# Ending and beginning the sub-layers of a two-layer decoder token tile by token tile

## The chip, the core and the metric

The kernel runs on one core of a Trainium2 chip. Its time is the device time in microseconds (us) of one execution. The core has a matrix engine (TensorE, PE in the profile; its weight loads are PEld), a vector engine (VectorE, DVE), a scalar engine (ScalarE, ACT), GpSimd (POOL) and SyncE (SP), which here starts the loads of the weights. The engines run side by side and wait for each other by semaphores. TensorE's results go to PSUM, which has eight banks here: three of them take transposes and small products, five take accumulators.

## The reference

Two layers on 256 tokens of width 2048, all in f32. Every sub-layer is wrapped in the same way, and that wrapping is what the change is about:

```
for i in range(DEPTH):
    h = rms_norm(x, g[0])
    mix = mlstm_mixer(h, ...) if i == 0 else gdn_mixer(h, ...)
    x = x + rms_norm(mix, g[1])
    h = rms_norm(x, g[2])
    x = x + rms_norm(mem_cross_attn(h, k_m, v_m, w_xq[i], w_xo[i]), g[3])
    h = rms_norm(x, g[4])
    x = x + rms_norm(sq_relu_mlp(h, w_up[i], w_down[i]), g[5])
```

`rms_norm(x, g)` is x * rsqrt(mean(x*x) + 1e-6) * g over the 2048 columns of a token. The mixer of layer 0 is an mLSTM, that of layer 1 a gated DeltaNet (gdn); each ends in a product with its output weights (m_out, g_out). The cross attention has four heads of 128 over 256 fixed memory tokens (products xq and xo), the MLP computes relu(h @ w_up)^2 @ w_down with 8192 inner columns (up and down).

## The kernel before

The 256 tokens are two tiles of 128 (t = 0 and 1). The residual stream x lies token-major in four chunks `xk` of 512 columns, each with both tiles. What goes into a product is feature-major: 16 tiles `h` of 128 features, each with 256 tokens twice, a high part and the rest (low part), since an f32 product is made of three products of rounded operands: high by high, high by low, low by high.

Weights come in units of 512 rows by 512 columns (four blocks of 128 rows), in the order of a plan. SP loads a unit in two halves (`raw`), ACT rounds each half into `hi` (L89) and VectorE makes the rest `lo` (L90). A product takes the units one after the other; `take` has the next ones started some units ahead, and the scheduler places these casts among the other work of ACT and VectorE, by program order, by a priority offset (`ws.first`) and by `behind(a, b)`, which keeps instruction a after b on their engine. After that order is set, each engine runs its instructions strictly in it.

There are two kinds of products. `prod_tok` (L384 to L386) keeps tokens on the output partitions and 512 columns free: three matmuls of 512 columns for each block of 128 rows and token tile. `prod_feat` (L318, L319, or L322 to L324 in the narrow form) keeps features on the partitions and tokens free; `prod_tall` (L337 to L339) is the same with one column of 128 features at a time. xq, up, and gdn's gq and gk are feature-major, xo, down, m_out, g_out and gdn's gz are token-major. The narrow form of three matmuls of 256 columns is used for xq, gq and the first four blocks of up (`fresh`), since it needs the high part of h first; the wide form is one matmul of 512 columns and one of 256.

A sub-layer ends in `Post`. `take` receives each accumulator of the last product as it is ready: ACT squares it (L232, the sum goes to `ss`), VectorE multiplies by the gain g into `y` (L472, L479); with down and g_out an earlier part of the sum is added first (L455). After the last chunk of a token tile `rstd` makes 1/rms: a reduction, a root on ACT and a reciprocal (L485 to L491). Then `advance` begins the next sub-layer. For each of the four chunks `residual` (L496) adds y * r to xk for both tiles, `feed` transposes the chunk's eight 128 by 128 blocks into two PSUM banks (L214) and splits them into h, ACT the high part (L249, 256 columns: both tiles), VectorE the low part (L250), in the two banks in turn; then ACT squares xk for the next norm (L232, junk<-xk), and two weight units are cast in between. The scale 1/rms of the next norm isn't applied to h: it is applied to the results later.

`extra_unit` puts the second of the next product's first two units into tiles that are free at the time (`xw` in the profile). In gdn the products gq, gk and gz alternate for four groups of heads; gz's results for the later heads go through memory (z_d). In the last sub-layer the output is written from xk.

## Time and profile before

| what | before |
|---|---|
| median of 3 runs | 2910.2 us (2903.45 to 2910.87) |
| profiled execution, its time | 2910.01 us |
| span of the profiled execution | 2908.3 us |
| granted TensorE clock, mean | 0.994 |
| busy: PE / DVE / ACT / POOL | 2867.1 / 1758.4 / 1425.2 / 158.4 us |

The page gives busy times, the chain of work that ended last, and the costliest groups of instructions. A row of a group is line, engine, operation, output<-inputs, shape and count, then busy time and mean duration (ns) of one, then the engine's idle time before them and what ended it. A row of a timeline is start, duration, engine, line, operation, tiles, shape, count, and in brackets the idle time before it with its releaser. A row of the waits is who waited for whom, the sum in us, the times and the longest. A row of a table of stretches is the stretch, its length, the busy time (and count) of PE, PEld, DVE, ACT and POOL, the granted clock, and the DMA share and rate. A matmul's duration overlaps that of its neighbours, so its pace is read from starts.

### The profile page before, as it was taken

The page shows a single profiled execution, that of the slowest core. Times are in us where ns is not written, and L with a number is a line of the kernel's source. Part 1 is how long each engine was busy: PE and PEld are TensorE (multiplying, and loading weights), DVE is VectorE, ACT ScalarE, POOL GpSimd, SP SyncE. Part 2 cuts the span into 40 slices and gives each one's busy share as a digit, 9 for nine tenths or more (in the row PEclk, how much of TensorE's full clock was granted, in tenths as well). Part 3 has the DMA queues.
Part 4 walks back from the last instruction along what each step waited for, and adds up shares of the span by engine and source line. Part 5 has one row for each costly group of instructions (what it writes and reads, how often), then busy time and mean ns, then how long its engine had stood idle before and what let it go on. Part 6 is the DMA issues. An engine that isn't in the chain of part 4 may idle for free.

```text
span 2908.3 us, 42466 instructions
## 1 busy us (share of the span) xinstructions
PE 2867.1 (99%) x16683; PEld 2478.4 (85%) x16683; DVE 1758.4 (60%) x2603; ACT 1425.2 (49%) x2125; POOL 158.4 (5%) x341
## 2 busy tenths in 40 slices
PE   8999999999999999999999999999999999999998
PEld 7888888888888888798998998888888888888887
DVE  5555656654645555577776895555576545455565
ACT  6444546544434444466664554544465444344443
POOL 0000000000000000002211114230000000000000
PEclk9999999999999999999999999999999999999999
DMA  7645564555555565658778777664545555655554
GB/s 239 193 145 174 189 201 144 191 188 189 188 191 188 192 194 184 214 154 238 228 214 242 207 221 238 206 207 163 200 158 168 188 191 187 197 186 194 190 188 167
DMA packets 379515, 562.40 MB, mean 193 GB/s; under 512 B 24593, under 2 KB 158994, under 8 KB 376882
## 3 DMA queue, kind: packets, MB, share of 16 engines
q1 hardware_dynamic: 363456, 507.12, 55.6%
q0 software_dynamic: 14288, 51.23, 5.2%
q8 instruction: 131, 2.15, 0.3%
q10 hardware_dynamic: 1570, 1.33, 0.1%
q14 instruction: 70, 0.57, 0.1%
HBM read 534.37 MB, written 25.23 MB: 192 GB/s over the span
## 4 chain that ended last, share of the span: by engine, by line
PE 91%; DVE 4%; DMA 2%; ACT 2%; issue 1%; DVEq 0%; SPq 0%; ACTq 0%
PE up L318 15%; PE up L319 8%; PE down L385 8%; PE down L384 8%; PE down L386 8%; PE g_out L386 2%; PE g_out L384 2%; PE g_out L385 2%; PE o L318 2%; PE gz L384 2%; PE gz L386 2%; PE gz L385 2%; DMA raw<-in_gdn_w_in 1%; DVE lo L90 1%; PE o L319 1%; PE v L386 1%
## 5 line engine op out<-in xcount | busy, mean ns | idle before, releaser
L90 DVE TENSOR_TENSOR lo<-raw,hi 128x1024 fp32r<-128x1024 f32 x938 | 1110.3, 1218 | 890.3 <-ACT hi L89 888.8
L89 ACT CAST hi<-raw 128x1024 fp32r<-128x1024 f32 x938 | 943.3, 1046 | 953.5 <-PE down L386 310.8
L318 PE MATMUL up<-h,hi 128*128 128x512 f32 x1920 | 678.7, 399 | 0.0
L319 PE MATMUL up<-h,lo 128*128 128x256 f32 x1920 | 539.2, 281 | 0.0
L318 PEld LDWEIGHTS up<-h,hi 128*128 128x128 f32 x1920 | 360.8, 188 | 89.9
L385 PE MATMUL down<-lo,u 128*128 128x512 f32 x1024 | 398.4, 389 | 0.0
L384 PE MATMUL down<-hi,u 128*128 128x512 f32 x1024 | 398.4, 389 | 0.0
L386 PE MATMUL down<-hi,u 128*128 128x512 f32 x1024 | 398.3, 389 | 0.0
L319 PEld LDWEIGHTS up<-h,lo 128*128 128x128 f32 x1920 | 362.7, 189 | 0.2
L384 PEld LDWEIGHTS down<-hi,u 128*128 128x128 f32 x1024 | 192.2, 188 | 40.1
L386 PEld LDWEIGHTS down<-hi,u 128*128 128x128 f32 x1024 | 192.2, 188 | 40.0
L385 PEld LDWEIGHTS down<-lo,u 128*128 128x128 f32 x1024 | 192.2, 188 | 39.6
L337 PE MATMUL gv<-h,hi 128*128 128x256 f32 x512 | 146.4, 286 | 2.5 <-ACT hi L89 2.5
L339 PE MATMUL gv<-h,lo 128*128 128x256 f32 x512 | 145.9, 285 | 0.9 <-DVE lo L90 0.9
L338 PE MATMUL gv<-h,hi 128*128 128x256 f32 x512 | 145.4, 284 | 0.0
L384 PE MATMUL gz<-hi,h 128*128 128x512 f32 x256 | 104.6, 409 | 0.0
L385 PE MATMUL gz<-lo,h 128*128 128x512 f32 x256 | 102.8, 402 | 0.0
L386 PE MATMUL gz<-hi,h 128*128 128x512 f32 x256 | 102.7, 401 | 0.0
L337 PEld LDWEIGHTS gv<-h,hi 128*128 128x128 f32 x512 | 98.7, 193 | 3.0 <-ACT hi L89 2.7
L339 PEld LDWEIGHTS gv<-h,lo 128*128 128x128 f32 x512 | 98.7, 193 | 1.2 <-DVE lo L90 1.1
L338 PEld LDWEIGHTS gv<-h,hi 128*128 128x128 f32 x512 | 98.6, 193 | 0.2 <-issue 0.2
L889 DVE SCALAR_TENSOR_TENSOR cv<-pad,cols,cv 128x256 f32<-128x256 f32 x192 | 90.8, 481 | 6.9 <-ACT cv L887 4.2
(435 smaller groups left out, 4701.5 us busy)
## 6 DMA issues: line engine op xcount, KB each, us to landing
raw<-in_w_up SPq DMA_DIRECT2D x256, 512.0 KB, 4.0
raw<-in_w_down SPq DMA_DIRECT2D x256, 512.0 KB, 4.1
raw<-in_gdn_w_in SPq DMA_DIRECT2D x192, 512.0 KB, 4.9
raw<-in_mlstm_w_in SPq DMA_DIRECT2D x96, 512.0 KB, 4.0
raw<-in_gdn_w_out SPq DMA_DIRECT2D x64, 512.0 KB, 4.4
raw<-in_mlstm_w_out SPq DMA_DIRECT2D x32, 512.0 KB, 4.5
at_d<-at POOLq DMA_DIRECT2D x8, 1536.0 KB, 7.9
ab<-at_d POOLq DMA_DIRECT2D x8, 1536.0 KB, 8.4
```

Of the source, the lines that this page charges most:

```text
L89: a = nc.scalar.copy(h_, raw[:, :, :n])
L90: return a, nc.vector.tensor_tensor(l_, raw[:, :, :n], h_, ALU.subtract)
L318: PE.matmul(a[:fw], wh, srcs[kk][:, :], start=(kk == 0), stop=False, skip_group_check=True)
L319: PE.matmul(a[:fw, T:], wl, srcs[kk][:, 0:T], start=False, stop=(kk == nk - 1), skip_group_check=True)
L337: PE.matmul(a[:, 0:T], hi[k], srcs[k][:, 0:T], start=(k == 0), stop=False)
L338: PE.matmul(a[:, 0:T], hi[k], srcs[k][:, T:], start=False, stop=False)
L339: m = PE.matmul(a[:, 0:T], lo[k], srcs[k][:, 0:T], start=False, stop=(k == nk - 1))
L384: PE.matmul(accs[t], sh, hi[j], start=(kk == 0), stop=False)
L385: PE.matmul(accs[t], sh, lo[j], start=False, stop=False)
L386: PE.matmul(accs[t], sl, hi[j], start=False, stop=(kk == nk - 1))
L889: V.scalar_tensor_tensor(c, pad[:, j : j + T], w[j], c, ALU.mult, ALU.add)
```

## The change

`advance` is gone; its work is spread over the end of one product and the beginning of the next. The last two weight units of the ending product are run as a pair: token tile 0 through both, then tile 1 through both. When tile 0 is done, its 1/rms is made (one sum of the first three chunks is taken earlier, and the root reads the last square's sum with that as its bias), and two residuals follow. `ahead` puts the transposes and splits of chunk 0, tile 0 into the middle of the last unit of tile 1; then come the remaining weight cast and chunk 1, tile 0. The first product of the next sub-layer is token-major now (xq with 384 columns, up with its first 512 columns, gz in gdn, moved ahead of gq), and its first two units are a pair again; after each of its four parts `between` places more: chunk 0 of tile 1, chunk 1 of tile 1, chunk 2 of both, chunk 3 of both. The results of xq and of the first up columns are transposed afterwards (xqt, and `feed` of utok). `half` transposes the four blocks of a chunk and one tile into one bank and splits them in 128 columns each. `follow` fixes the order on ACT and VectorE around it. The eight squares of xk stand after the last split. Besides, weight casts get a priority offset of 60 around xo, the load of the root's table is asked for earlier, and the exponential of gdn's a_log stands behind the lead.

```diff
+        steps = [(c, k) for c in range(n_ch) for k in range(0, nk, UK)]
+        accs, units = {}, {}
+        def fetch(i):
+            c, k = steps[i]
+            if k == 0:
+                if start:
+                    start(c)
                 for t in range(2):
+                    accs[c, t] = acc(f"{key}{c}_{t}")
+            units[i] = ws.take(key, 1 if post and i == len(steps) - 1 or lead and i < 2 else None)
+        def run(i, t, j0=0, j1=UK):
+            c, k = steps[i]
+            hi, lo, kb, n = units[i]
+            a = accs[c, t][:, :n]
+            for j in range(j0, j1):
+                kk = k + j
+                sh, sl = srcs[kk][:, t * P : (t + 1) * P], srcs[kk][:, T + t * P : T + (t + 1) * P]
+                PE.matmul(a, sh, hi[j][:, :n], start=(kk == 0), stop=False)
+                PE.matmul(a, sh, lo[j][:, :n], start=False, stop=False)
+                PE.matmul(a, sl, hi[j][:, :n], start=False, stop=(kk == nk - 1))
+        def done(i, t):
+            c, k = steps[i]
+            if k + UK == nk:
+                evac(c, t, accs[c, t][:, : units[i][3]])
+        pairs, i = [], 0
+        while i < len(steps):
+            two = i == 0 and lead or i == len(steps) - 2 and (post or split)
+            pairs.append((i, i + 1) if two else (i,))
+            i += len(pairs[-1])
+        for p_ in pairs:
+            last = p_[-1] == len(steps) - 1
+            if post and last:
+                extra_unit(4 if nk == UK else 0)
+            for i in p_:
+                fetch(i)
             for t in range(2):
+                for i in p_:
+                    if t and i == p_[-1] and last and post:
+                        post.halves = ws.begin()
+                        run(i, t, 0, UK // 2)
+                        post.ahead()
+                        run(i, t, UK // 2)
+                    else:
+                        run(i, t)
+                    if lead and p_[0] == 0:
+                        lead.between(t * 2 + i)
+                    done(i, t)
+            if after:
+                for i in p_:
+                    after(steps[i][1] // UK)
...
+            if ch == 2:
+                p_ = self.pre[t] = small.tile([P, 1], F32, tag=f"pre{t}", name="pre")
+                self.later(V.tensor_reduce(p_, self.rms.ss[:, t, 0:3], AX.X, ALU.add))
+                V.scalar_tensor_tensor(p_, p_, 1.0 / D, self.bias[:, t : t + 1] if self.bias is not None else eps_t,
+                                       ALU.mult, ALU.add)
             if ch == 3:
-                self.r.append(self.rstd(t))
-                late = lambda: V.tensor_tensor(d, a, self.g[ch], ALU.mult)
-                if t == 0 and not plus:
-                    late()
-                else:
-                    self.late.append(late)
-                self.added = v if plus else None
+                r = self.r[t] = small.tile([P, 1], F32, tag=f"rpost{t}", name="rpost")
+                S.activation(r, self.rms.ss[:, t, 3:4], AF.Sqrt, bias=self.pre[t], scale=1.0 / D)
+                self.invert = lambda: V.reciprocal(r, r)
+                if not self.nxt or t == 0:
+                    self.invert()
+                self.late = lambda: V.tensor_tensor(d, a, self.g[ch], ALU.mult)
+                if self.nxt and t == 0:
+                    self.residual(0, 0)
+                    self.first = self.residual(1, 0)
+                    self.late()
...
+        def half(self, ch, t):
+            p_ = psum(f"lth{ch}")
+            for i in range(4):
+                PE.transpose(p_[:, i * P : (i + 1) * P], xk[ch][:, t, i * P : (i + 1) * P], ident)
+            for i in range(4):
+                kb = ch * 4 + i
+                if t == 0:
+                    self.h[kb] = acts.tile([P, 2 * T], F32R, tag=f"h{kb}", name=f"h{kb}")
+                g_, d, s_ = gain(*self.nxt, kb), self.h[kb], p_[:, i * P : (i + 1) * P]
+                a = S.activation(d[:, t * P : (t + 1) * P], s_, AF.Copy, scale=g_)
+                v = V.scalar_tensor_tensor(d[:, T + t * P : T + (t + 1) * P], s_, g_, d[:, t * P : (t + 1) * P],
+                                           ALU.mult, ALU.subtract)
+                self.follow(a, v)
+        def follow(self, a, v):
+            if self.last:
+                behind(a, self.last[0])
+                behind(v, self.last[1])
+            self.last = a, v
+        def both(self, ch):
+            for t in range(2):
+                behind(self.residual(ch, t), self.halved)
+            self.h[ch * 4 : ch * 4 + 4] = [acts.tile([P, 2 * T], F32R, tag=f"h{kb}", name=f"h{kb}")
+                                           for kb in range(ch * 4, ch * 4 + 4)]
+            return feed(xk[ch], ch, self.h, lambda k: gain(*self.nxt, k))
+        def ahead(self):
+            self.follow(*self.halves.pop(0)())
+            self.half(0, 0)
+        def advance(self):
+            if self.added:
+                behind(self.added, self.last[1])
+                self.last = self.last[0], self.added
+            for half in self.halves:
+                self.follow(*half())
+            self.half(1, 0)
+            self.x_rms = Rms("x")
+            return self
+        def between(self, i):
+            if i < 2:
+                if i == 0:
+                    behind(self.invert(), self.last[1])
+                behind(self.residual(i, 1), self.last[1])
+                self.half(i, 1)
+                if i == 1:
+                    self.halved = self.last[1]
+                    behind(self.late(), self.halved)
+                    ws.prefetch(1, self.follow)
+            elif i == 2:
+                self.both(2)
             else:
...
-        return h, rms
+                a, _ = self.both(3)
+                for ch in range(4):
+                    for t in range(2):
+                        behind(self.x_rms.add(xk[ch][:, t, :], t, ch), a)
...
+        qtok = [sc.tile([P, 384], F32, tag=f"qtok{t}", bufs=1, name="qtok") for t in range(2)]
+        prod_tok("xq", h, 1, lambda c, t, a: (V.tensor_copy, S.copy)[t](qtok[t], a), after=scales, lead=lead)
+        for f in range(XA_H - 1):
+            p_ = psum("xqt")
+            for t in range(2):
+                PE.transpose(p_[:, t * P : (t + 1) * P], qtok[t][:, f * P : (f + 1) * P], ident)
+            ev_q(f, Bank(p_, False))
...
+        S.sqrt(warm, sums[-1][:, 0:1])
+        ws.first = 60
+        lead = out_proj("xo", o, l, 3, (l, 4), True)
+        ws.first = 0
+        return lead
...
+        def first(ch, t, a):
+            S.activation(d[:, t, :], a, AF.Relu)
+            V.scalar_tensor_tensor(d[:, t, :], a, 0.0, d[:, t, :], ALU.max, ALU.mult)
         for c in range(NQ):
+            if c == 0:
+                prod_tok("up", h, 1, first, lead=lead)
             u = new_u()
-            prod_feat("up", h, KB, relu2(u), fresh=c == 0)
+            if c == 0:
+                feed(d, 0, u, lambda k: None)
+            prod_feat("up", h, KB, relu2(u), f0=0 if c else 4)
...
+            early_z(0, lead)
+            behind(S.activation(na, na, AF.Exp), lead.last[0])
...
-                early_z(c)
+                if c < 3:
+                    early_z(c + 1)
```

How it moves the instructions, first at the end of m_out in layer 0. On ACT before (junk<-m_out are the last squares of m_out's tiles 0 and 1, rpost the root, h the high parts from the banks ltp, junk<-xk the squares of x, hi74 and hi75 weight casts):

```order
L232 ACTIVATE junk_3851,sspost_3255<-m_out3_0_3697 128x512 [waits PE_49]
L487 ACTIVATE rpost_3855<-rpost_3855,eps_t_87 128x1 [waits DVE_49]
L232 ACTIVATE junk_3860,sspost_3255<-m_out3_1_3698 128x512 [waits PE_49]
L487 ACTIVATE rpost_3862<-rpost_3862,eps_t_87 128x1 [waits DVE_49]
L249 ACTIVATE h0_3868<-ltp0_3887,cols_98 128x256 [waits PE_49]
L249 ACTIVATE h2_3870<-ltp2_3888,cols_98 128x256 [waits PE_49]
L249 ACTIVATE h1_3869<-ltp0_3887,cols_98 128x256 [waits DVE_49]
L249 ACTIVATE h3_3871<-ltp2_3888,cols_98 128x256 [waits DVE_49]
L232 ACTIVATE junk_3906,ssx_3867<-xk0_108 128x512
L232 ACTIVATE junk_3908,ssx_3867<-xk0_108 128x512 [waits Activation_49]
L89 CAST hi74_3821<-raw74_2_3825 128x2x384 [waits DMAHW3_49]
L249 ACTIVATE h4_3872<-ltp4_3920,cols_98 128x256 [waits PE_49]
```

and now (lth is the bank of a half):

```order
L236 ACTIVATE junk_3827,sspost_3255<-m_out3_0_3703 128x512 [waits PE_49]
L503 ACTIVATE rpost_3829<-sspost_3255,pre_3681 128x1 [waits Activation_49]
L89 CAST hi74_3847<-raw74_0_3849 128x2x384 [waits DMAHW2_49,DVE_49,PE_49]
L536 ACTIVATE h0_3866<-lth0_3861,cols_98 128x128 [waits PE_49]
L536 ACTIVATE h1_3869<-lth0_3861,cols_98 128x128 [waits DVE_49]
L236 ACTIVATE junk_3884,sspost_3255<-m_out3_1_3704 128x512 [waits PE_49]
L536 ACTIVATE h2_3872<-lth0_3861,cols_98 128x128 [waits DVE_49]
L503 ACTIVATE rpost_3886<-sspost_3255,pre_3699 128x1 [waits Activation_49]
L536 ACTIVATE h3_3875<-lth0_3861,cols_98 128x128 [waits DVE_49]
L89 CAST hi74_3847<-raw74_2_3851 128x2x384 [waits DMAHW3_49]
L536 ACTIVATE h4_3895<-lth1_3890,cols_98 128x128 [waits PE_49]
L536 ACTIVATE h5_3898<-lth1_3890,cols_98 128x128 [waits DVE_49]
```

The splits are 128 columns wide and four to a bank, and each after the first of a bank waits for VectorE; the square and root of tile 1 stand among those of tile 0, and the squares of x are no longer between the chunks. On VectorE at the same place now (h are the low parts, xk the residuals):

```order
L507 TENSOR_TENSOR y3_3254<-m_out3_0_3703,g3_3551 128x512 [waits Activation_49]
L504 RECIPROCAL rpost_3829<-rpost_3829 128x1 [waits Activation_49]
L524 SCALAR_TENSOR_TENSOR xk0_108<-y0_3251,rpost_3829,xk0_108 128x512 [waits DVE_49]
L524 SCALAR_TENSOR_TENSOR xk1_109<-y1_3252,rpost_3829,xk1_109 128x512
L90 TENSOR_TENSOR lo74_3848<-raw74_0_3849,hi74_3847 128x2x384 [waits DMAHW2_49,Activation_49]
L537 SCALAR_TENSOR_TENSOR h0_3866<-lth0_3861,cols_98,h0_3866 128x128 [waits Activation_49]
L537 SCALAR_TENSOR_TENSOR h1_3869<-lth0_3861,cols_98,h1_3869 128x128 [waits Activation_49]
L537 SCALAR_TENSOR_TENSOR h2_3872<-lth0_3861,cols_98,h2_3872 128x128 [waits Activation_49]
L537 SCALAR_TENSOR_TENSOR h3_3875<-lth0_3861,cols_98,h3_3875 128x128 [waits Activation_49]
L90 TENSOR_TENSOR lo74_3848<-raw74_2_3851,hi74_3847 128x2x384 [waits DMAHW3_49,Activation_49]
L537 SCALAR_TENSOR_TENSOR h4_3895<-lth1_3890,cols_98,h4_3895 128x128 [waits Activation_49]
L537 SCALAR_TENSOR_TENSOR h5_3898<-lth1_3890,cols_98,h5_3898 128x128 [waits Activation_49]
```

Every low part waits for the high part of the same block on ACT; the two residuals of tile 0 come before the first of them.

The second place is the end of xo in layer 0, on ACT, where up's weight unit 86 is cast. Before (squares of the last chunks, the last splits h12 to h15, the casts of units 85 and 86):

```order
L232 ACTIVATE junk_4652,ssx_4553<-xk2_110 128x512 [waits Activation_49]
L232 ACTIVATE junk_4654,ssx_4553<-xk2_110 128x512 [waits Activation_49]
L89 CAST hi85_4804<-raw85_0_4806 128x1024 [waits DMAHW4_49,PE_49]
L249 ACTIVATE h12_4566<-ltp12_4657,cols_98 128x256 [waits PE_49]
L249 ACTIVATE h14_4568<-ltp14_4658,cols_98 128x256 [waits PE_49]
L89 CAST hi85_4804<-raw85_2_4808 128x1024 [waits DMAHW6_49]
L249 ACTIVATE h13_4567<-ltp12_4657,cols_98 128x256 [waits DVE_49]
L249 ACTIVATE h15_4569<-ltp14_4658,cols_98 128x256 [waits DVE_49]
L232 ACTIVATE junk_4675,ssx_4553<-xk3_111 128x512 [waits Activation_49]
L232 ACTIVATE junk_4677,ssx_4553<-xk3_111 128x512 [waits Activation_49]
L89 CAST hi86_4862<-raw86_0_4864 128x1024 [waits DMAHW7_49,PE_49]
L89 CAST hi86_4862<-raw86_2_4866 128x1024 [waits DMAHW0_49]
```

and now:

```order
L253 ACTIVATE h13_4709<-ltp12_4712,cols_98 128x256 [waits DVE_49]
L253 ACTIVATE h15_4711<-ltp14_4713,cols_98 128x256 [waits DVE_49]
L236 ACTIVATE junk_4730,ssx_4577<-xk0_108 128x512
L236 ACTIVATE junk_4732,ssx_4577<-xk0_108 128x512
L236 ACTIVATE junk_4734,ssx_4577<-xk1_109 128x512
L236 ACTIVATE junk_4736,ssx_4577<-xk1_109 128x512 [waits Activation_49]
L236 ACTIVATE junk_4738,ssx_4577<-xk2_110 128x512 [waits Activation_49]
L236 ACTIVATE junk_4740,ssx_4577<-xk2_110 128x512 [waits Activation_49]
L236 ACTIVATE junk_4742,ssx_4577<-xk3_111 128x512 [waits Activation_49]
L236 ACTIVATE junk_4744,ssx_4577<-xk3_111 128x512 [waits Activation_49]
L89 CAST hi86_4780<-raw86_0_4782 128x1024 [waits DMAHW7_49,PE_49]
L89 CAST hi86_4780<-raw86_2_4784 128x1024 [waits DMAHW0_49]
```

The eight squares now stand one after the other behind the last split, and the cast of unit 86 behind all of them; before, they stood two by two behind the splits of their own chunk, four of them ahead of the rows shown.

174 lines of the change are left out of this document (55 added, 119 removed).

## The prediction

> **What bounds the kernel now.** I read the page first, then the waits, then the stretches around the places where one sub-layer hands over to the next. The busy times by engine and the chain that ended last:
>
> ```profile
> PE 2867.1 (99%) x16683; PEld 2478.4 (85%) x16683; DVE 1758.4 (60%) x2603; ACT 1425.2 (49%) x2125; POOL 158.4 (5%) x341
> ...
> PE 91%; DVE 4%; DMA 2%; ACT 2%; issue 1%; DVEq 0%; SPq 0%; ACTq 0%
> ```
>
> TensorE sets the time. The change touches its work little, so what counts is where TensorE stands still: 9% of the chain, and mostly at the hand-overs. Let T be the time since the moment at which 24 matmuls (5.44 us) of the ending product are left. The five inner hand-overs, each from T = 0 to the first matmul of what follows unchanged (A: m_out to xo, B: xo to the second block of up, C: down to gk, D: g_out to xo, E: as B in layer 1), by stretches:
>
> ```profile
> 447.63:489.99 42.36, 40.51 (x282) 37.93 (x281) 31.54 (x66) 27.88 (x66) 0.00 (x0) 0.96 0.50 152
> 510.94:546.16 35.22, 32.80 (x250) 30.91 (x248) 28.57 (x52) 24.84 (x56) 0.00 (x0) 1.00 0.58 183
> 1228.15:1264.54 36.39, 33.18 (x253) 31.29 (x252) 25.77 (x46) 21.56 (x48) 0.00 (x0) 1.00 0.53 158
> 2111.09:2154.34 43.25, 40.23 (x282) 37.40 (x281) 32.89 (x68) 27.89 (x65) 0.00 (x0) 0.96 0.49 151
> 2175.43:2211.62 36.19, 34.25 (x250) 32.35 (x249) 28.71 (x52) 24.98 (x57) 0.00 (x0) 0.95 0.56 179
> ```
>
> The first number is the length, then PE, PEld, DVE, ACT; the one before the last two is the granted clock. DVE and ACT are busy for 59 to 81% of these 35 to 43 us: they have no great reserve there. Now A on TensorE (start, length, idle before and its releaser):
>
> ```profile
> 449.67 0.39 PE L384 MATMUL m_out<-hi,u 128*128 128x512 f32 x1
> ...
> 453.07 0.60 PE L214 MATMUL ltp<-ident,xk 128*128 128x128 f32 x4
> 455.52 1.10 PE L214 MATMUL ltp<-ident,xk 128*128 128x128 f32 x6 [1.85 <-DVE xk L496]
> ...
> 457.75 0.41 PE L323 MATMUL xq<-h,xw 128*128 128x256 f32 x1
> 457.97 0.41 PE L324 MATMUL xq<-h,xw 128*128 128x256 f32 x1
> ...
> 461.03 0.28 PE L322 MATMUL xq<-h,xw 128*128 128x256 f32 x1
> 461.15 0.28 PE L323 MATMUL xq<-h,xw 128*128 128x256 f32 x1
> ...
> 479.74 0.47 PE L337 MATMUL xq<-h,hi 128*128 128x256 f32 x1
> ```
>
> From 449.67 to 453.07 stand 15 matmuls of 512 columns, 0.2267 us each. TensorE then waits 1.85 us for the residual xk. What it runs next starts every 0.22 us, and every 0.12 us from 461.03 on: half clock for four microseconds after the gap. A, D and E have this (0.96, 0.96, 0.95), B and C don't (1.00). ACT and VectorE in the same place:
>
> ```profile
> 453.27 0.60 ACT L232 ACTIVATE junk<-m_out 128x512 f32<-128x512 f32 x1 [1.52 <-PE m_out L386]
> 454.18 0.29 ACT L487 ACTIVATE rpost<-rpost,eps_t 128x1 f32<-128x1 f32 x1 [0.22 <-DVE rpost L485]
> 455.99 0.84 ACT L249 ACTIVATE h<-ltp,cols 128x256 fp32r<-128x256 f32 x2 [1.51 <-PE ltp L214]
> 457.02 0.87 ACT L249 ACTIVATE h<-ltp,cols 128x256 fp32r<-128x256 f32 x2 [0.19 <-DVE h L250]
> 457.78 0.62 ACT L232 ACTIVATE junk<-xk 128x512 f32<-128x512 f32 x1
> ```
>
> ```profile
> 456.50 0.87 DVE L250 SCALAR_TENSOR_TENSOR h<-ltp,cols,h 128x256 fp32r<-128x256 f32 x2 [0.38 <-ACT h L249]
> 457.52 0.88 DVE L250 SCALAR_TENSOR_TENSOR h<-ltp,cols,h 128x256 fp32r<-128x256 f32 x2 [0.15 <-ACT h L249]
> 458.32 0.68 DVE L472 TENSOR_TENSOR y<-m_out,g 128x512 f32<-128x512 f32 x1
> 458.92 1.40 DVE L496 SCALAR_TENSOR_TENSOR xk<-y,rpost,xk 128x512 f32<-128x512 f32 x2
> ```
>
> Splitting one 512-column chunk of both token tiles takes from 455.99 to 458.40, 2.4 us, because two PSUM banks go to and fro: while ACT reads one, VectorE reads the other. That the two wait for each other in one bank, both ways, is in the waits, with the gap of TensorE below them:
>
> ```profile
> ACT h L249 <- DVE h L250: 10.8, 18, 1.1
> DVE h L250 <- ACT h L249: 8.4, 25, 1.2
> PE ltp L214 <- DVE xk L496: 11.8, 9, 2.2
> ```
>
> **The change, part by part.** *The narrow splits.* For chunks 0 and 1 each token tile now has a half of its own: four transposes into one bank, and from it four times an ACT row and a VectorE row of 128 columns. Each next ACT row waits for the VectorE row before it, as the order shows. The profile of before has no such row of h, so I take other rows of that size from PSUM, beside the weight casts that stand in the same queues:
>
> ```profile
> L668 ACT ACTIVATE dm<-ep,mg 128x128 f32<-128x128 f32 x12 | 3.5, 366 | 3.2 <-PE ep L665 3.1
> L1226 DVE SCALAR_TENSOR_TENSOR zs<-op,ss,zs 128x128 f32<-128x128 f32 x64 | 17.7, 344 | 0.9
> L90 DVE TENSOR_TENSOR lo<-raw,hi 128x768 fp32r<-128x768 f32 x12 | 11.3, 956 | 5.4 <-ACT hi L89 5.1
> L90 DVE TENSOR_TENSOR lo<-raw,hi 128x1024 fp32r<-128x1024 f32 x938 | 1110.3, 1218 | 890.3 <-ACT hi L89 888.8
> L89 ACT CAST hi<-raw 128x1024 fp32r<-128x1024 f32 x938 | 943.3, 1046 | 953.5 <-PE down L386 310.8
> ```
>
> A step is 0.366 + 0.344 us and two hand-overs of about 0.035 (an ACT row of 0.47 from 455.99 ends at 456.46, VectorE starts at 456.50), 0.78 us. A half is four steps, 3.1 us; four halves 12.5 us, where two chunks took 4.8 in two banks. Bounds: 0.40 if the two overlapped, and 1.02 if a row of 128 cost as much as one of 256 (two L249/L250 rows of 0.47). I take 0.78, nearest in size; 16 steps in five hand-overs make 80 steps, so the ends are -30 and +19 us on the sum.
>
> *Hand-over A.* The early part gains: token tile 0 is normalised while TensorE still has tile 1 to do. The square (0.2 to 0.88 with its read-out), the root directly behind it (1.21), y3 (0.68), the reciprocal and the first residual (0.75) are through at T = 2.4, so the first transposes wait for nothing; they stand behind 18 matmuls, at 4.08. From there the halves set the pace: tile 0 of chunk 0, with the square and root of tile 1 in between on ACT, to 8.3; the rest of weight unit 74 and chunk 1 to 12.3; residual and chunk 0 of tile 1 to 16.9; residual and chunk 1 to 21.4. Then y3 0.68, two low parts of 0.95 that partly ran before, four residuals 2.7: 26.4. Chunks 2 and 3 as before, 5.8: 32.2. TensorE has 96 matmuls of 384 columns to lay under this (about 0.174 us each, midway between 0.12 and 0.2267: 16.7 us, 0.6 less than the 144 narrow ones of before) and waits at every half. Now comes what is late next: all eight squares of x stand on ACT behind the last split, 8 x 0.62 less a little overlap, 4.9 us, from about 31.6 to 36.5, and behind them the cast of weight unit 77 (1.0, to 37.5) and its low part on VectorE (1.2, to 38.8). The third xq product needs both. Before it began at 479.74, T = 32.1, so 6.7 us are lost, and six more transposes (0.11 each) add 0.7: **+7.4**. The same squares feed the scale of the softmax, so nothing behind can run past them.
>
> *B.* The same chain, with the wider up block (96 x 0.2267 = 21.8 us, 1.35 less than 192 x 0.12) beneath: last split at 35.3, TensorE through at 38.3, but the next block waits for unit 86, queued on ACT behind the squares (34.75 + 4.9 + 1.04 = 40.7; low part 41.97). TensorE goes on from about 41.5, with 8 more transposes (0.86) 42.3, against 35.2: **+7.1**. *E* likewise 42.3 against 36.2: **+6.1**. *D* as A with the additions of g_out's chunks, 50.0 against 43.25: **+6.8**. *C* begins with gz in place of gq, 1.4 us less work; the product ends at 39.8, then waits 1.1 for the reciprocal root behind two squares and a table load: 40.9 against 36.4 - 1.4 = 35.0, **+5.9**. Its store of z goes with it on POOL's queue (5% busy, nobody waits for it until the output gate). The exponential of a_log, put behind the lead, adds one table load on ACT after the splits; ACT's 49% hide it, at most 1.3 if not. In gdn the last head group loses gz as cover and has about 8 us of VectorE work under the v products: VectorE's 40% idle hides it; -2 to +2, I take 0.
>
> *Weights of xo.* The first two units are now cast earlier. What that can give is the stall in xo:
>
> ```profile
> 504.01 0.39 PE L386 MATMUL xo<-hi,u 128*128 128x512 f32 x1
> 504.54 0.73 PE L384 MATMUL xo<-hi,u 128*128 128x512 f32 x2
> 505.80 0.50 PE L385 MATMUL xo<-lo,u 128*128 128x512 f32 x1 [0.52 <-DVE lo L90]
> ```
>
> Three matmuls take from 504.01 to 505.80, 1.8 us where 0.7 is due, and the fourth is 0.11 longer than its neighbours' 0.39: -1.2, once in each layer, **-2.4**. *The output's tail* loses a reduction and a small product between the last square and the residuals (0.16 + 0.15 and two hand-overs of 0.1): **-0.5**.
>
> Sum: 7.4 + 7.1 + 5.9 + 6.8 + 6.1 - 2.4 - 0.5 = +30.4. Against the profiled execution's 2910.0 (the median of the runs is 2910.2) that is **2940 us**.
>
> **The clock.** I leave the half clock as it is in the rows: some 1.7 us in three of five hand-overs. The Trainium skill's "TensorE: Matmul & The Clock Gate", Part 1, says the clock halves after an idle window of about 3.4 us and needs as much activity to come back; in A 1.85 us of waiting, or 3.45 with the transposes on both sides, was followed by the slow rows, while B and C, with the same order of work, stayed at 1.00, so the rows agree on the length of the slow stretch and show no fixed trigger. By that rule a hand-over with matmuls in every window would never cool, and the sum would be 5 us lower.
>
> **Rivals.** *Overlap (no change).* If the 128-column rows overlap after all, each hand-over gets 6.2 us back: 2909. For it: only the order says that they don't. Against: the waits of 10.8 and 8.4 us in both directions.
>
> *The gaps decide (faster).* If the halves never hold TensorE and the squares aren't in the way, the 11.8 us of waiting for xk, 5 us of half clock and 2.9 us of xo and tail go, and 1 to 2 us of work: about 2888. It decides if a half takes under the 2.1 us of twelve 384-column matmuls that lie beside it. 3.1 speaks against it, and the reserve of ACT and VectorE too.
>
> *Only the feed.* If the casts of units 77 and 86 run before the squares, or the products hold enough other work, some 3.3 us of each hand-over drop out: 2940 - 17 = 2923. For it: TensorE has attention work in A and D. Against: on ACT the squares stand first.
>
> *A cold clock.* If waits at every half keep TensorE at half clock, the first products take 16.7 to 21.8 us more, less what they waited anyhow: A and D +5 over my sum, B, C and E +10, together 2980. For it: 0.22 us after a gap of 1.85. Against: C, 1.00 after its gaps.
>
> **How the numbers follow.** Forecast 0.59, only the feed 0.15, the gaps decide 0.12, overlap 0.08, cold clock 0.06. 0.3%, 8.7 us, is what can be told from no change here. Faster: 0.12. Same: overlap and a little of the feed's low side, 0.10. Slower: 0.78. The forecast's own range is 2926 to 2956. To leave out no more than 2 in 10 the low end goes to 2907, which takes in the feed and the overlap; the high end stays at 2957, short of the cold clock and about the dear step (2959).
>
> **What would show it.** Right: waits of the ACT h row on the VectorE h row in the new half, 2 us and more per half; ltp or lth transposes that no longer wait for xk; the third xq product and the second up block waiting for hi or lo behind eight squares in a row; stretches A to E some 6 to 7 us longer; no wait for lo in xo. Wrong: steps well under 0.78 us, TensorE busy through the halves, or a granted clock near 0.5 through the first product. It falls as a whole if the halves end before their matmuls need them.

## The result

The change made the kernel slower: 2942.0 us (median of 4 runs, 2939.7 to 2944.1) against 2908.1 us (4 runs, 2903.5 to 2910.9), a ratio of 1.0118 with a 95% interval of 1.0100 to 1.0135. The forecast was 2940, in a range of 2907 to 2957. The profiled execution of the changed kernel took 2942.3 us. Its page, busy times and chain of waits:

```profile
PE 2884.7 (98%) x16423; PEld 2465.4 (84%) x16423; DVE 1766.9 (60%) x2649; ACT 1437.6 (49%) x2163; POOL 158.4 (5%) x341
...
PE 88%; DVE 6%; ACT 3%; issue 1%; DMA 1%; DVEq 0%; ACTq 0%
```

TensorE's share of the chain fell from 91 to 88%, VectorE's and ACT's rose from 6 to 9% together: the time went into waits of TensorE for these two. To see where, both executions are cut at the same points: A from T = 0 at the end of m_out to T = 0 at the end of xo, D the same in layer 1; B from there to the first matmul of down, E the same in layer 1; C from T = 0 at the end of down to the second gq. Before, these stretches were 63.3, 103.1, 99.1, 64.3 and 104.0 us. The table of stretches after (stretch, length, busy PE, PEld, DVE, ACT, POOL, granted clock, DMA share, GB/s):

```profile
446.16:521.63 75.47, 67.45 (x331) 54.41 (x330) 48.27 (x94) 44.76 (x102) 0.20 (x4) 0.95 0.40 121
521.63:631.54 109.91, 104.23 (x542) 84.96 (x541) 69.55 (x117) 57.39 (x108) 0.00 (x0) 0.97 0.56 172
1245.69:1372.80 127.11, 119.93 (x710) 102.87 (x708) 81.21 (x153) 73.23 (x121) 7.46 (x18) 0.95 0.56 165
2127.13:2201.11 73.98, 65.51 (x331) 53.38 (x330) 49.42 (x96) 44.79 (x102) 0.00 (x0) 0.98 0.41 121
2201.11:2312.19 111.08, 105.40 (x543) 85.47 (x541) 69.98 (x117) 57.66 (x108) 0.00 (x0) 0.97 0.55 172
sum 497.55, PE 462.53 PEld 381.09 DVE 318.42 ACT 277.82 POOL 7.65; mean PE 92.51 PEld 76.22 DVE 63.68 ACT 55.56 POOL 1.53
```

and the sum of the same table before:

```profile
sum 433.82, PE 419.79 PEld 373.15 DVE 299.77 ACT 253.84 POOL 6.35; mean PE 83.96 PEld 74.63 DVE 59.95 ACT 50.77 POOL 1.27
```

After the change C holds one gz product more, which before came later: 96 matmuls at 0.2267 us, 21.8 us. Without it the five stretches take 475.8 us, 42 more than before: A +12.2, B +6.9, C +6.3, D +9.6, E +7.1. The rest of the kernel gave 10 us back: the middle of gdn, from the second gq on, about 7.7, the start of the kernel up to m_out's end 1.5 and the output's tail 0.5. The span grew by 32.2.

The halves, in hand-over A. Chunk 0 of token tile 1 on ACT, then what follows the last split (rows of ACT's timeline after):

```profile
459.95 0.37 ACT L536 ACTIVATE h<-lth,cols 128x128 fp32r<-128x128 f32 x1 [1.99 <-PE lth L530]
460.74 0.37 ACT L536 ACTIVATE h<-lth,cols 128x128 fp32r<-128x128 f32 x1 [0.42 <-DVE h L537]
...
478.80 0.62 ACT L236 ACTIVATE junk<-xk 128x512 f32<-128x512 f32 x1
...
483.09 0.61 ACT L236 ACTIVATE junk<-xk 128x512 f32<-128x512 f32 x1
...
483.70 1.03 ACT L89 CAST hi<-raw 128x1024 fp32r<-128x1024 f32 x1
...
485.77 0.47 ACT L848 COPY qtok<-xq 128x384 f32<-128x384 f32 x1
```

VectorE in the same half:

```profile
460.35 0.35 DVE L537 SCALAR_TENSOR_TENSOR h<-lth,cols,h 128x128 fp32r<-128x128 f32 x1 [1.15 <-ACT h L536]
461.14 0.35 DVE L537 SCALAR_TENSOR_TENSOR h<-lth,cols,h 128x128 fp32r<-128x128 f32 x1 [0.43 <-ACT h L536]
```

One row of 128 columns on ACT, one on VectorE, in turn: 0.79 us from one ACT row to the next, where 0.78 was forecast. Over the whole kernel, by groups and by waits:

```profile
L536 ACT ACTIVATE h<-lth,cols 128x128 fp32r<-128x128 f32 x80 | 29.4, 368 | 48.5 <-DVE h L537 26.4 <-PE lth L530 22.0
L537 DVE SCALAR_TENSOR_TENSOR h<-lth,cols,h 128x128 fp32r<-128x128 f32 x80 | 28.0, 350 | 38.9 <-ACT h L536 38.9
```

And TensorE at the end of the same hand-over (start, length, idle before and its releaser):

```profile
467.71 0.36 PE L386 MATMUL xq<-hi,h 128*128 128x384 f32 x1
470.63 1.95 PE L218 MATMUL ltp<-ident,xk 128*128 128x128 f32 x10 [2.55 <-DVE xk L524]
472.30 0.69 PE L384 MATMUL xq<-hi,h 128*128 128x384 f32 x1
...
484.78 0.39 PE L339 MATMUL xq<-h,hi 128*128 128x256 f32 x1 [1.47 <-ACT hi L89]
...
486.04 0.58 PE L341 MATMUL xq<-h,lo 128*128 128x256 f32 x1 [0.75 <-DVE lo L90]
...
488.13 0.41 PE L340 MATMUL xq<-h,hi 128*128 128x256 f32 x1
488.34 0.41 PE L341 MATMUL xq<-h,lo 128*128 128x256 f32 x1
...
489.18 1.02 PE L832 MATMUL xs<-kmT,xq 128*128 128x256 f32 x4
```

The reader sees three things here: a wait of 2.55 us for the residual of chunk 2; the forecast wait for weight unit 77 behind the eight squares (1.47 for hi, 0.75 for lo); and the first scores xs, which start at 489.18, that is T = 43.0, where before they started at T = 30.6 (478.20 in the trace of before). A wait of the first kind is TensorE's longest in each of the five hand-overs. Over the whole kernel:

```profile
PE ltp L218 <- DVE xk L524: 16.4, 6, 4.5
PE lth L530 <- DVE xk L524: 2.2, 7, 0.5
```

Before, TensorE waited 11.8 us for xk; now it waits 18.6, most of it ahead of chunk 2, 2.5 to 4.5 us in each hand-over.

### The profile page after: what moved, and what is told of

It is laid out like the page before. It is cut to its first block, busy times and chain, and to the rows that moved or that the text cites. A ratio compares the mean times of both kernels' runs of the same rounds, so it can differ in the third digit from the quotient of the medians.

```text
span 2940.5 us, 42023 instructions
## 1 busy us (share of the span) xinstructions
PE 2884.7 (98%) x16423; PEld 2465.4 (84%) x16423; DVE 1766.9 (60%) x2649; ACT 1437.6 (49%) x2163; POOL 158.4 (5%) x341
## 4 chain that ended last, share of the span: by engine, by line
PE 88%; DVE 6%; ACT 3%; issue 1%; DMA 1%; DVEq 0%; ACTq 0%
PE up L320 15%; PE down L386 8%; PE down L385 8%; PE down L384 8%; PE up L321 8%; PE g_out L386 2%; PE g_out L384 2%; DVE lo L90 2%; PE g_out L385 2%; PE o L320 2%; PE gz L384 2%; PE gz L386 2%; PE gz L385 2%; PE o L321 1%; PE v L386 1%
## 5 line engine op out<-in xcount | busy, mean ns | idle before, releaser
L386 PEld LDWEIGHTS down<-hi,u 128*128 128x128 f32 x1024 | 192.2, 188 | 39.9
L384 PE MATMUL gz<-hi,h 128*128 128x512 f32 x248 | 101.5, 409 | 0.5 <-ACT h L536 0.5
L386 PE MATMUL gz<-hi,h 128*128 128x512 f32 x248 | 99.4, 401 | 0.4 <-DVE h L537 0.4
```

The lines of the kernel that those rows point to most:

```text
L384: PE.matmul(a, sh, hi[j][:, :n], start=(kk == 0), stop=False)
L386: PE.matmul(a, sl, hi[j][:, :n], start=False, stop=(kk == nk - 1))
```

## The experiments

The kernel before ran beside each on the same chip: 2907.6 us (25 runs) with the first four, 2909.9 us (7 runs) with the last three. Stretches below are those of the table above, C without the additional gz product where there is one. Single executions of one kernel differ by up to 9 us on either side of the median, so stretches say where time lies, medians how much it is. The profiled execution of both edits was the fastest of its ten, 8.8 us under their median. The change itself was run only beside the kernel before at 2908.1 us; set against the kernel before that ran beside each, the gains of the last three over the change are some 2 us larger than the medians as they stand.

| us | A | B | C | D | E | sum | median |
|---|---|---|---|---|---|---|---|
| before | 63.3 | 103.1 | 99.1 | 64.3 | 104.0 | 433.8 | 2907.6, 2909.9 |
| the change | 75.5 | 109.9 | 105.3 | 74.0 | 111.1 | 475.8 | 2942.0 |
| two banks | 68.0 | 105.3 | 96.8 | 67.2 | 103.9 | 441.1 | 2906.5 |
| squares spread | 71.7 | 108.6 | 104.9 | 70.6 | 107.6 | 463.4 | 2928.8 |
| banks and squares | 63.8 | 103.5 | 94.2 | 64.0 | 103.6 | 429.1 | 2901.6 |
| xq copied by VectorE | 72.4 | 108.9 | 105.1 | 72.1 | 110.4 | 468.8 | 2932.6 |
| cast first | 72.9 | 109.0 | 105.7 | 72.8 | 110.1 | 470.5 | 2935.4 |
| all, early residuals | 61.8 | 102.2 | 96.3 | 64.0 | 100.9 | 425.2 | 2891.3 |

### A half in two banks

```diff
-            p_ = psum(f"lth{ch}")
-            for i in range(4):
-                PE.transpose(p_[:, i * P : (i + 1) * P], xk[ch][:, t, i * P : (i + 1) * P], ident)
+            p_ = [psum(f"lth{ch}{b}") for b in range(2)]
+            for i in (0, 2, 1, 3):
+                PE.transpose(p_[i % 2][:, i // 2 * P : (i // 2 + 1) * P], xk[ch][:, t, i * P : (i + 1) * P], ident)
...
-                g_, d, s_ = gain(*self.nxt, kb), self.h[kb], p_[:, i * P : (i + 1) * P]
+                g_, d, s_ = gain(*self.nxt, kb), self.h[kb], p_[i % 2][:, i // 2 * P : (i // 2 + 1) * P]
```

> The change as it is, but a half spreads its four blocks over two PSUM banks, so that ACT and VectorE can each read one. Theory (the to and fro in one bank is on the path): a half falls from 3.1 to 1.9 us (0.37 + 0.37 on ACT beside 0.35 on VectorE), four halves from 12.5 to 7.6; beside the first products' matmuls (2.1 us for twelve of 384 columns, 2.7 for twelve of 512) some 3.5 to 4.5 us of each of the five hand-overs come back: 2920 to 2925 us. Rival (only the squares and casts behind the feed hold TensorE): no more than 3 us in all, 2939 to 2942.

Measured: 2906.5 us (10 runs, 2902.7 to 2910.3), ratio to before 0.9995 (0.9985 to 1.0005). This one edit takes back 35 us, all that the change had lost, where 17 to 22 were expected. The five stretches still take 7 us more than before; what the change gained elsewhere, gdn's order above all, makes up for them. The same half on ACT:

```profile
459.18 0.62 ACT L536 ACTIVATE h<-lth,cols 128x128 fp32r<-128x128 f32 x2 [1.58 <-PE lth L530]
459.96 0.62 ACT L536 ACTIVATE h<-lth,cols 128x128 fp32r<-128x128 f32 x2 [0.16 <-DVE h L537]
```

and on VectorE:

```profile
459.58 0.61 DVE L537 SCALAR_TENSOR_TENSOR h<-lth,cols,h 128x128 fp32r<-128x128 f32 x2 [0.93 <-ACT h L536]
460.36 0.61 DVE L537 SCALAR_TENSOR_TENSOR h<-lth,cols,h 128x128 fp32r<-128x128 f32 x2 [0.18 <-ACT h L536]
```

Two rows in a row take 0.62 us, not two times 0.37, and the half lasts from 459.18 to 460.97, 1.8 us where it was 3.1 (459.95 to 463.06). Twenty halves make 26 us. The sum of the stretches fell by 34.7. Much of the remainder is likely the granted clock, which rose in all five stretches, from 0.95 to 0.97 in A and from 0.98 to 1.00 in D for two: 1 minus the clock, times the length, summed over the five, is 18 us after the change and 10 here, by which I estimate 8 us. No run separates it. The waits within the halves, who for whom, sum, times and longest:

```profile
DVE h L537 <- ACT h L536: 14.2, 30, 1.2
ACT h L536 <- DVE h L537: 5.5, 18, 1.0
```

Those of ACT for VectorE fell from 26.4 us, those the other way from 38.9. TensorE's wait for xk fell with them, from 16.4 and 2.2 us to

```profile
PE ltp L218 <- DVE xk L524: 9.3, 5, 2.0
```

The rival, that only what stands behind the feed counts, is out.

### The squares spread

```diff
...
+            self.square(0, 0)
+            self.square(1, 0)
...
+                if i == 0:
+                    self.square(0, 1)
...
+                    self.square(1, 1)
...
-                self.both(2)
+                a, _ = self.both(2)
+                for t in range(2):
+                    behind(self.x_rms.add(xk[2][:, t, :], t, 2), a)
...
-                for ch in range(4):
-                    for t in range(2):
-                        behind(self.x_rms.add(xk[ch][:, t, :], t, ch), a)
+                for t in range(2):
+                    behind(self.x_rms.add(xk[3][:, t, :], t, 3), a)
```

> The change as it is, but the squares of x stand where ACT waits: two behind the halves of token tile 0, one behind each half of tile 1, two behind the splits of chunk 2, and only the last two behind the last split. Theory (the casts of the next weight unit and the scale of the softmax wait behind eight squares): casts and scale come 3.7 us earlier in each of five hand-overs, 2924 to 2928 us. Rival (what follows would wait as long for something else): within 3 us of the change, 2939 to 2943.

Measured: 2928.8 us (4 runs, 2927.1 to 2931.2), ratio 1.0072 (1.0053 to 1.0092): 13 us under the change, just short of the 14 to 18 of the theory. The stretches fell by 12.4, A, D and E by 3.4 to 3.8, but B by 1.3 and C by 0.4. So the squares are on the path, and not evenly. In E the granted clock was 1.00 here and 0.97 in the change, 3% of 111 us, so most of E's 3.5 us may be the clock; B, the same place in the other layer, gained 1.3.

### Both edits

> Both edits together, two banks and spread squares. If the two waits stand one behind the other in the chain, their gains add: 2903 to 2911 us. If one hides the other, the better of the two alone, some 2920.

The two diffs together. Measured: 2901.6 us (10 runs, 2892.8 to 2905.1), ratio 0.9973 (0.9961 to 0.9985), 40 us under the change. The single edits gave 35 and 13, 48 together. By the medians the second edit is worth 4.9 us on top of the first, where it was worth 13 alone. The stretches fell by 34.7, 12.4 and 46.7, almost the sum, but this profiled execution was 8.8 us under the median of its runs, so its stretches look better than the kernel is. And that 2901.6 lies near the range for gains that add doesn't decide, for this range was made with 17 to 22 us for the first edit and not 35. So the second wait isn't wholly hidden by the first, as 2906.5 would have it, and it isn't wholly behind it either: some 8 us of it are gone once the halves are short. Why is open.

### Only gdn's gz products moved, on the kernel before

```diff
             for c in range(4):
                 ws.add("gq", g_in, 0, D, c * 512, 512, tall=c > 0)
+                if c == 0:
+                    ws.add("gz", g_in, 0, D, GDN_QKV + 2048, 512)
...
-                ws.add("gz", g_in, 0, D, GDN_QKV + 2048 + c * 512, 512)
+                if c < 3:
+                    ws.add("gz", g_in, 0, D, GDN_QKV + 2560 + c * 512, 512)
...
+                if c == 0:
+                    early_z(0)
                 prod_k(c)
...
-                early_z(c)
+                if c < 3:
+                    early_z(c + 1)
```

> The kernel before with one thing of the change: gdn's gz products move one place ahead (the first directly behind gq, so that none stands behind the fourth group's gk), all hand-overs as before. Theory from the two traces (the projections of gdn took 7.8 us less after the change because of this order): 2900 us, -8. Rival, the prediction's (VectorE's idle time hides the order either way): 2906 to 2910.

Measured: 2900.9 us (10 runs, 2896.8 to 2907.2), ratio 0.9979 (0.9967 to 0.9990): 6.8 us faster than before. This part of the change pays, and the prediction had it at nothing. The first lines of the edit move the loads of the weights with the products. Where the time went: all of gv (first row) and the fourth group's stretch (second row), before,

```profile
1564.60:1762.64 198.04, 193.29 (x1597) 192.38 (x1596) 163.11 (x262) 95.11 (x142) 22.85 (x60) 0.99 0.81 232
1488.47:1564.60 76.13, 76.13 (x529) 70.32 (x527) 54.89 (x86) 45.52 (x60) 12.91 (x30) 1.00 0.76 217
```

and in this kernel, the fourth group first:

```profile
1503.27:1552.42 49.15, 49.15 (x407) 48.62 (x405) 39.88 (x65) 33.33 (x45) 7.29 (x19) 1.00 0.85 233
1552.42:1750.10 197.68, 196.73 (x1624) 194.66 (x1622) 166.48 (x275) 97.04 (x145) 27.13 (x69) 1.00 0.79 232
```

The fourth group takes 76.1 - 21.8 - 49.2 = 5.2 us less, since work of its pairs now runs within gv (1624 against 1597 matmuls there), and gv is no longer for it: TensorE stood idle for 4.75 us in it before (198.04 - 193.29) and for 0.95 now. Near the end of gv before, the longest wait of ACT is 6.7 us for one transfer of gdn's weights; TensorE waited 2.5 us for hi and 0.9 for lo there, and its granted clock was 0.87 in the last 13 us. In this kernel the wait for hi is gone and the clock there was 1.00. Why that transfer ends better in the new order was not tried. The second group of heads also took 5.6 us less in this profiled execution (78.88 against 84.47, granted clock 1.00 against 0.96), but only 2.4 less in that of the change, so this part may be chance.

### xq copied out by VectorE alone

```diff
-        prod_tok("xq", h, 1, lambda c, t, a: (V.tensor_copy, S.copy)[t](qtok[t], a), after=scales, lead=lead)
+        prod_tok("xq", h, 1, lambda c, t, a: V.tensor_copy(qtok[t], a), after=scales, lead=lead)
```

> The change as it is, but both token tiles of the first xq product are copied out of PSUM by VectorE; in the change ACT copies the second one, behind two weight casts. The scheduler then also puts the first head's scores ahead of the third xq product. Theory (in the two hand-overs to the cross attention the excess over the prediction, some 6 and 4 us, is the softmax that starts late): the first scores come some 5 us earlier; bounded by their scale, which waits for the squares, 3 to 5 us in each of the two, 2932 to 2936 us. Rival (the third xq product and its weights alone set the delay): 2939 to 2943.

Measured: 2932.6 us (4 runs, 2930.1 to 2934.6), ratio 1.0079 (1.0064 to 1.0094), 9.4 us under the change. The first scores in A:

```profile
485.02 1.13 PE L832 MATMUL xs<-kmT,xq 128*128 128x256 f32 x4 [0.52 <-DVE xq L425]
```

They start at T = 38.6 (T = 0 at 446.40) and not at 43.0. A shrank by 3.1 and D by 1.9 in the profiled executions; B, C and E, which the edit doesn't touch, by 2.1 together. So the direction is shown and its size is between 5 us by the two stretches and 9 to 11 us by the medians.

### The cast ahead of the squares

```diff
-                a, _ = self.both(3)
+                self.last = self.both(3)
+                ws.prefetch(2)
+                ws.prefetch(3, self.follow)
                 for ch in range(4):
                     for t in range(2):
-                        behind(self.x_rms.add(xk[ch][:, t, :], t, ch), a)
+                        behind(self.x_rms.add(xk[ch][:, t, :], t, ch), self.last[0])
```

> The change as it is, but the cast of the next weight unit (77 or 86) stands between the last split and the eight squares. Theory (in the hand-overs to up and gdn the cast behind the squares is all that TensorE waits for, in those to the attention the scale counts too): 3 to 4 us from each of two, perhaps three hand-overs, 0 to 2 from the two others, 2926 to 2934 us. If the cast alone decides everywhere: 2922 to 2926. If neither, 2939 to 2943.

Measured: 2935.4 us (4 runs, 2931.6 to 2940.7), ratio 1.0090 (1.0073 to 1.0107), 6.6 us under the change, with 9 us between its own four runs: a miss. The gain isn't where it was expected: A 2.6, D 1.2, B and E 1 each, C none. The reason stands in the trace of the change, in hand-over B on TensorE, where the token-major part of up ends and the feature-major part begins:

```profile
563.48 0.39 PE L386 MATMUL up<-hi,h 128*128 128x512 f32 x1
563.70 0.84 PE L320 MATMUL up<-h,hi 128*128 128x512 f32 x3
564.65 0.39 PE L321 MATMUL up<-h,lo 128*128 128x256 f32 x1
```

The last token-major matmul starts at T = 41.9 (T = 0 at 521.63), not at 38. Unit 86 is late too, as forecast: its cast begins at 562.30, behind the squares, but that is early enough for its high part, and its low part costs some 0.4 us only (the four matmuls from 563.70 on take 1.17 us to the next, 0.8 at the pace of those that follow). TensorE is late by itself: the last 48 of its 96 matmuls there, 10.9 us, need chunks 2 and 3 of h, which come behind the four halves.

### Two banks, spread squares, VectorE's copies and earlier residuals

```diff
-                behind(self.residual(i, 1), self.last[1])
+                r = self.residual(i, 1)
+                behind(r, self.last[1])
+                behind(self.residual(i + 2, 0), r)
...
-                    self.halved = self.last[1]
+                    self.halved = self.residual(2, 1)
+                    behind(self.halved, self.last[1])
...
-            for t in range(2):
-                behind(self.residual(ch, t), self.halved)
+            if ch == 3:
+                behind(self.residual(ch, 1), self.halved)
```

> Two banks and spread squares together with VectorE's copies of xq, and the residuals of chunks 2 and 3 moved ahead: those of token tile 0 directly behind tile 1's residuals of chunks 0 and 1, that of chunk 2, tile 1 directly behind the halves, ahead of a gain product and two low parts. With two banks and spread squares TensorE still waits 2.0 us for xk before chunk 2 in most hand-overs. If that wait is on the path: 1.5 to 2 us in each of five, and 1 to 3 from the copies: 2890 to 2895 us, 6 to 11 under the two-bank kernel with spread squares. If what follows is bound by VectorE's total work there: 2900.

Measured: 2891.3 us (4 runs, 2886.7 to 2892.3), ratio 0.9934 (0.9920 to 0.9949). The stretches of this kernel, with the granted clock before the last two numbers:

```profile
446.36:508.12 61.76, 60.04 (x328) 51.14 (x327) 48.52 (x96) 43.20 (x101) 0.20 (x4) 1.00 0.48 146
508.12:610.35 102.23, 101.23 (x546) 84.61 (x544) 68.99 (x116) 56.38 (x108) 0.00 (x0) 1.00 0.58 187
1224.49:1342.50 118.01, 116.16 (x710) 102.02 (x708) 80.46 (x152) 71.94 (x121) 7.43 (x18) 0.97 0.61 178
2095.21:2159.25 64.04, 61.58 (x332) 52.41 (x330) 48.99 (x98) 43.09 (x101) 0.00 (x0) 1.00 0.45 139
2159.25:2260.15 100.90, 99.20 (x542) 83.70 (x541) 68.68 (x117) 56.73 (x108) 0.00 (x0) 1.00 0.59 190
```

It is faster than both kernels, 18.6 us under before and 51 under the change, and 10 under the two edits alone. In none of the five hand-overs a wait of TensorE for xk is left, and the granted clock is 1.00 in A, B, D and E. That fits a wait for the residual that is on the path, but doesn't show its price: the copies and the residuals were not run apart, and in B, C and E, which the copies don't touch, the stretches are 1.3 less, 2.1 more and 2.7 less than with the two edits. If the gains add, about 7 of the 18.6 are gdn's new order, as the fourth experiment has it, and some 11 are for the hand-overs, once their waits are mended. The kernel before with its own waits mended was not run, so it isn't shown that these 11 need the new form.

## Why the prediction was right, and where it was not

**What bounds the kernel, and the sign.** Right. What decided was not TensorE's work but the to and fro of ACT and VectorE in one bank. The step was forecast at 0.78 us and is 0.79, with 0.368 and 0.350 us for the rows, where 0.366 and 0.344 were taken from other rows of the same size. The waits of ACT for VectorE were 1.3 us a half (26.4 over twenty), not the "2 us and more" given as a sign; three gaps of 0.42, as the step itself has it. The Trainium skill's "PSUM — Partial Sum Buffer", section on bank collisions, says that ScalarE and VectorE may not access one bank at the same time on the same quarter of the partitions, reads against reads included, and that different banks run clean. The waits here agree: those of ACT for VectorE, which only the bank asks for (a high part takes nothing from the low part before it), were 26.4 us in one bank and 5.5 in two.

**The overlap bound and its rival.** The bound "0.40 if the two overlapped" was near: in two banks a half takes 1.8 us, 0.45 a step, so the halves by themselves give back 26 us, where the bound had 30. The kernel got 35, the rest likely from the clock, which the term didn't have. The overlap rival put its time at 2909, and with overlap the chip gave 2906.5; but gdn's order, 7 us that the rival didn't have either, stands in that, so the nearness is partly luck. Its mechanism is the one that the first experiment switches on.

**TensorE's wait for xk.** One sign of being right failed: "ltp or lth transposes that no longer wait for xk". The early ones hardly do, 2.2 us in seven waits, but those of chunk 2 wait longer than any did before. The sum had the four residuals in its chain; what it didn't draw from them is that TensorE has run out of work by then and stands still. The rival in which the gaps decide needed these waits to go, and they grew from 11.8 to 18.6 us.

**Hand-over A, +7.4, and D, +6.8.** Too low: with xo they are +12.2 and +9.6, against +6.2 and +5.6 forecast. The step that failed is "The third xq product needs both. Before it began at 479.74, T = 32.1, so 6.7 us are lost": the delay was priced at the third xq product, but the longer chain is the first scores, 12.4 us later than before, since ACT copies xq behind two casts, and the scores stand on TensorE behind fifteen matmuls of the third product. That product itself began where it was forecast, at T = 38.6 for hi and 39.9 for lo against 38.8. Its fifteen matmuls were slow besides: from 484.78 to 489.18 the granted clock was 0.61. The fifth experiment, which changes that copy, got 5 to 11 us back, where A and D together lie 10 above their forecast.

**Hand-overs B, +7.1, and E, +6.1.** The sums were right, at +6.9 and +7.1. The steps were not: "TensorE through at 38.3, but the next block waits for unit 86". TensorE was through at 42.1, and the wait for unit 86 was 0.4 and not 3.2. The work that needs chunks 2 and 3, 10.9 us of it, had been laid under the halves in good part; it can't lie there. The sixth experiment bears it out: with the cast ahead of the squares B and E gain 1 us each.

**Hand-over C, +5.9.** Measured +6.3 in one pair of executions; C varies by several us from one to the next, so this confirms the sign only.

**gdn's order, 0 with a band of 2.** Wrong: -7.7 in the profiled pair, -6.8 by the fourth experiment. The step that failed is "VectorE's 40% idle hides it". It did hide it: TensorE was busy for all of the 49.15 us of the shorter fourth group. What was overlooked is that TensorE had 4.75 us of idle time in gv before, 3.4 of them waits for weights near the end; of all this 0.95 is left in the new order.

**xo, -2.4.** TensorE's idle time in xo was 0.66 us in each layer (before, first row; 22.28 of 22.28 us busy after, second row):

```profile
489.82:510.94 21.12, 20.46 (x91) 15.63 (x90) 14.23 (x22) 13.45 (x26) 0.00 (x0) 1.00 0.38 123
```

```profile
499.35:521.63 22.28, 22.28 (x100) 17.85 (x101) 14.79 (x25) 13.81 (x28) 0.20 (x4) 1.00 0.38 120
```

The stall went, as forecast, and is worth 0.7 and not 1.2 us; the stretch grew, because nine matmuls of the late attention moved into it.

**The tail, -0.5.** Right: from the last addition to the residuals 2.77 us before, 2.28 after.

**The clock.** "I leave the half clock as it is" was too kind. The first 33 us of B and of E after the change:

```profile
521.63:554.96 33.33, 27.76 (x112) 18.75 (x111) 24.03 (x48) 16.23 (x36) 0.00 (x0) 0.90 0.48 151
2201.11:2234.38 33.27, 27.69 (x113) 18.69 (x111) 24.14 (x48) 16.50 (x36) 0.00 (x0) 0.90 0.48 157
```

A mean of 0.90 is a fifth of the 33 us at half clock, and it lies in one place. In B the granted clock was 1.00 from 521.63 to 547.00, through all four halves with TensorE's waits at every step, and 0.50 to 0.54 from there to 554.20, with the wait for the residual of chunk 2 (3.04 us) and behind it. So the rival of the cold clock had the wrong mechanism: waits at every half left the clock as it was, and the half clock came with one longer gap, in all five hand-overs of the change. In A no product ran between 467.71 and 472.30, only a wait of 2.55 us and ten transposes; the clock was granted at 0.50 in the 3.2 us that followed:

```profile
472.30:475.47 3.17, 3.17 (x11) 2.60 (x10) 2.42 (x6) 1.51 (x4) 0.00 (x0) 0.50 1.04 271
```

The Trainium skill's "TensorE: Matmul & The Clock Gate", Part 4, says that transposes don't count as activity the way products do. This stretch agrees; no run here has transposes alone. With two banks the wait is 2.0 us in four of the five, and the half clock came in three of those four.

So the total, 2 us off, is partly luck: the hand-overs were 11 us dearer than their terms, gdn's order gave 8 us that had no term, and the start of the kernel 1.5.

## What to carry to other kernels

When two engines take turns in one PSUM bank, the price of a step is the sum of both rows and both hand-overs, and narrower rows make it worse: give each engine a bank of its own before cutting work finer. A gap of TensorE can cost twice, as the wait and as the slow stretch behind it: here 3.0 us, and then some 7 us at half clock. Work that nobody seems to wait for, as the squares here, still holds whatever is queued behind it on its engine: place it where that engine already waits. And price a delay at every chain that starts from the late result, with the work that can't begin before it, not at the first instruction that stands next in line.

## What the runs showed that was not expected

Rows of 128 columns on ACT, one behind the other without a wait, take 0.31 us each (0.62 for two) where one alone takes 0.37. Waits of half a microsecond at every step, with TensorE busy for 85% of the time, left the granted clock at 1.00 (532 to 544 in B of the change); one wait of 2.5 us or more ahead of eight or ten transposes was followed by half clock every time. And executions of one kernel lay up to 13 us apart (2902.3 to 2915.2 for the kernel before in 25 runs), which is more than several of the edits here move.
